# Seven products of a feed-forward pair: two PSUM regions that accumulate in turn, copied out by ScalarE in between

## The chip, the cores and the metric

The kernel runs on one core of one Trainium2 chip. The core's engines are TensorE (PE, matmuls; its weight loads are listed as PEld), VectorE (DVE), ScalarE (ACT), GpSimd (POOL) and SyncE (SP, which issues the DMAs here). The metric is the device time of one execution in microseconds (us), lower is better. Products are accumulated in PSUM, which has eight banks of 512 float32 columns per partition.

## The reference

A trunk of two layers over 512 tokens of width 1024 in float32. Each layer runs four sublayers with residuals: a feed-forward block, a mixer (gated DeltaNet in the first layer, Mamba2/SSD in the second), a cross attention to 256 memory rows, and a second feed-forward block. The change is in the feed-forward block, of which there are four:

```python
def swiglu(x, w_in, w_out):
    gate, up = jnp.split(x @ w_in, 2, axis=-1)
    return (jax.nn.silu(gate) * up) @ w_out
...
    u = swiglu(rms_norm(h, g[0, 0]), ffn_w_in[l, 0], ffn_w_out[l, 0])
    h = h + MACARON_W * rms_norm(u, g[0, 1])
```

`w_in` is 1024 x 5632 (gate and up of 2816 hidden columns each), `w_out` 2816 x 1024.

## The kernel before

Float32 operands are split into two float32r parts, `hi` and `lo`, that add up to them; ACT makes `hi` by a copy and DVE makes `lo` by a subtraction (`weights`, L129 and L130; `split`, L137 and L138). Each product is then three matmuls (`mm3`, L143 to L145: hi x hi, hi x lo, lo x hi) for each block of 128 rows.

The hidden columns of a feed-forward block come in 22 pairs of a gate and an up block of 128 columns. Pairs 0 and 1 use plain products (`plain`). The other 20 use `pair` (L473), which saves one product in eight in the manner of Strassen and Winograd: with the tokens in two halves of 256 (L, H), the 1024 rows in two halves (a, b) and gate and up as the two halves of the columns, seven products of halves give all four results. The sums of normalised rows that they need (`S1` to `S4`) are made once per block in `enter`; the sums of weights T1 to T4 are made per pair by DVE (L485, L486, L487, L489) and split (`T14`, `T23`). One product is four blocks of rows times three matmuls, twelve matmuls of 128x256 (`product`, L406).

In `pair` the products go to halves of four PSUM banks: X (tag a) takes A12 and A11, V (tag f) S2, Z (tag a) S4 and S3, Y (tag a) S1 and A22. Tag a has three banks, tag f one, s and c two each (`bank`, L113). ACT copies one result out (L502, `s5`); DVE adds the others up in SBUF:

```python
        nc.scalar.copy(self.s5, X[:, L])
        add(gt[:, L], self.s5, X[:, H])
...
        add(u2, self.s5, V[:, L])
        add(v, u2, Y[:, L])
        add(u3, u2, Z[:, H])
        sub(gt[:, H], u3, Y[:, H])
...
        add(c2(up), c2(Z), v.unsqueeze(1).broadcast_to([P, 2, 256]))
        nc.scalar.activation(gt, gt, AF.Silu)
        nc.vector.tensor_mul(gt, up, gt)
```

These are L502 to L513; then `put_hidden` splits the result (L468, L469).

Weight tiles come through three raw buffers, and five buffers each for `hi` and `lo`. `rest` (L540) walks the pairs; behind most of them it steps a generator, `slices` (L516), that multiplies two finished hidden blocks with the output weights: a chunk of 24 matmuls of 512 columns into the banks of tags s and c, for which the thresholds in `todo` decide (none behind pairs 5, 7 and 9). The order of instructions on each engine follows from dependences and from priorities that rise in the order in which the program is traced; `later` (L103) shifts the priority of a part, and `pair` has no shift.

Of the kernel before, what the change touches and what calls it, by code (L numbers as in the profile page):

```python
# [17 lines left out]
P = 128  # L18
# [43 lines left out]
class Trunk:  # L62
# [39 lines left out]
    @contextmanager  # L102
    def later(self, n):  # L103
        """what is traced here gives way to the next n instructions"""
        n = LATER.get(n, 0)
        self.tc.cur_priority += n
        yield
        self.tc.cur_priority -= n
# [4 lines left out]
    def bank(self, tag):  # L113
        """a PSUM bank: a for the long products, f, s and c for the mixers' chains"""
        return self.pm.tile([P, T], F32, name="ps_" + tag, tag=tag, bufs={"a": 3, "f": 1}.get(tag, 2))

    def weights(self, src, pool=None, nt=4):
        """a tile of weights in two float32r parts that add up to it"""
        nc = self.nc
        n = src.shape[1]  # L120
        raw = self.wp.tile([P, D], F32, name="raw", tag="raw", bufs=3)
        if pool is None:
            hi = self.wp.tile([P, D], F32R, name="whi", tag="whi", bufs=5)
            lo = self.wp.tile([P, D], F32R, name="wlo", tag="wlo", bufs=5)
        else:
            hi = pool.tile([P, D], F32R, name="thi", tag="thi", bufs=nt)
            lo = pool.tile([P, D], F32R, name="tlo", tag="tlo", bufs=nt)
        nc.sync.dma_start(out=raw[:, :n], in_=src)
        nc.scalar.copy(hi[:, :n], raw[:, :n])  # L129
        nc.vector.tensor_sub(lo[:, :n], raw[:, :n], hi[:, :n])  # L130
        return hi, lo
# [9 lines left out]
    def mm3(self, ps, lhs, rhs, first, last):  # L141
        mm = self.nc.tensor.matmul
        mm(ps, lhs[0], rhs[0], start=first, stop=False)  # L143
        mm(ps, lhs[0], rhs[1], start=False, stop=False)  # L144
        mm(ps, lhs[1], rhs[0], start=False, stop=last)  # L145
# [6 lines left out]
    def heads(self, srcs, half, st, outer=False):  # L152
        """the first products of a phase, for half of the tokens, block by block of the rows as they come"""
        if half == 0:
            st["w"] = [self.weights(x) for x in srcs]
            st["ps"] = [self.bank(x) for x in "aaaf"]
        s = slice(half * 256, half * 256 + 256)
        n = range(len(srcs))
        with self.later(0 if half else 'head'):
            for k, i in [(k, i) for i in n for k in range(KB)] if outer else [(k, i) for k in range(KB) for i in n]:  # L160
                kk = slice(k * P, k * P + P)
                w, ps = st["w"][i], st["ps"][i]
                self.mm3(ps[:, s], (w[0][:, kk], w[1][:, kk]), (self.xh[:, k, s], self.xl[:, k, s]),
                         k == 0, k == KB - 1)

    def out_weights(self, src, fh, pool=None, nt=4):
        """[[hi, lo] of each block of 128 rows] for 512 output columns"""
        res = []
        for kp in range(src.shape[1]):
            hi, lo = self.weights(src[fh, kp], pool, nt)  # L170
            for n in range(2):
                ns = slice(n * T, n * T + T)
                res.append((hi[:, ns], lo[:, ns]))
        return res

    def out(self, xs, ws, i, fh, first, last, tag):
        """u[tokens of tile i, columns of half fh] (+)= xs^T ws"""
        ps = self.bank(tag)
        ts = slice(i * P, i * P + P)
        for k, ((hi, lo), w) in enumerate(zip(xs, ws)):  # L180
            self.mm3(ps, (hi[:, ts], lo[:, ts]), w, k == 0, k == len(xs) - 1)
        nc = self.nc
        dst = self.u[:, i, fh * T:fh * T + T]
        if first:
            nc.scalar.copy(dst, ps)
        else:
            nc.vector.tensor_add(dst, ps, dst)
        if last:
            self.sumsq(dst, self.ssu[:, i, fh:fh + 1])
# [8 lines left out]
    def rcol(self, ss):  # L198
        """(mean of the squares + eps) ** -0.5, from the two sums of 512 squares"""
        nc = self.nc  # L200
        r = self.nt.tile([P, 1], F32, name="rcol", bufs=4)
        nc.vector.tensor_add(r, ss[:, 0:1], ss[:, 1:2])
        nc.scalar.activation(r, r, AF.Sqrt, bias=self.eps[:, 0:1], scale=1.0 / D)
        nc.vector.reciprocal(r, r)
        return r

    def warm(self, func, x):
        """the tables of func, loaded when x is there"""
# [10 lines left out]
    def post(self, i, square):  # L219
        """h += u * rsqrt(mean(u^2) + eps) * gain, and the sums of the squares of h"""  # L220
# [14 lines left out]
    def features(self, src, ss, g, hi, lo, ts, tag="c"):  # L235
        """the normalised rows of src [tokens, 1024], transposed, times gain g, in two parts"""
# [30 lines left out]
    def last_group(self, name, og, inner, ctx):  # L267
        """the last rows of a mixer's output projection, for the tail"""
# [12 lines left out]
    def conv(self, ps, dst, w):  # L281
        """causal taps along the tokens"""
# [6 lines left out]
    def small_proj(self, name, pool, tag, bufs):  # L289
        """the 32 columns of per-head values, [32, tokens]"""  # L290
# [10 lines left out]
    def rsqrt(self, pool, x, shape):  # L301
        """(x) ** -0.5 elementwise by Newton steps on a float32 guess; x is a small [P, n] view."""
# [12 lines left out]
    def softplus(self, pool, x, shape):  # L315
        """log1p(exp(x)) in place, as max(x, 0) + 2 atanh(e / (e + 2)) with e = exp(-|x|)."""
# [18 lines left out]
class FFN:  # L335
    """the input projection by seven products of halves (of the tokens, of the rows, gate and up) for eight"""
# [21 lines left out]
    def sums(self):  # L358
        """place for three sums of quarters of the normalised rows, in two parts"""
# [6 lines left out]
    def enter(self, i, ss, tag):  # L366
        """the normalised rows of tile i, and for the later half of the tokens the sums of quarters, in two parts"""
# [38 lines left out]
    def product(self, ps, w, x, first=True, last=True):  # L406
        """ps[feature, token] (+)= w^T x over four blocks of rows"""
        for k in range(4):
            kk = slice(k * P, k * P + P)
            self.t.mm3(ps, (w[0][:, kk], w[1][:, kk]), (x[0][:, k, :], x[1][:, k, :]), first and k == 0, last and k == 3)  # L410

    def early(self, n, ws, tags):
        """the first half of the tokens of a pair, by plain products"""
# [31 lines left out]
    def plain(self, n):  # L445
        """a pair of hidden blocks by eight products; the later half of the tokens from the sums of its quarters"""
# [26 lines left out]
    def pair(self, n):  # L473
# [5 lines left out]
        X = t.bank("a")  # L479
        for i, x in ((1, self.A12), (0, self.A11)):  # L480
            self.product(X[:, i * 256:i * 256 + 256], self.part(w, i), x)
        sub = nc.vector.tensor_sub
        T1, T4 = self.T14[:, a], self.T14[:, b]
        T2, T3 = self.T23[:, a], self.T23[:, b]
        sub(T1, u[:, a], g[:, a])  # L485
        sub(T2, u[:, b], T1)  # L486
        sub(T4, T2, g[:, b])  # L487
        w14 = t.split(self.T14)
        sub(T3, u[:, b], u[:, a])  # L489
        w23 = t.split(self.T23)  # L490
# [5 lines left out]
        up = t.nt.tile([P, T], F32, name="xs", bufs=2)  # L496
        add = nc.vector.tensor_add
        Z, Y, V = t.bank("a"), t.bank("a"), t.bank("f")
        u2, u3, v = self.s
        prods = [(V[:, L], half(w23, a), self.S2), (Z[:, L], b22, self.S4), (Y[:, L], half(w14, a), self.S1),  # L500
                 (Y[:, H], half(w14, b), self.A22), (Z[:, H], half(w23, b), self.S3)]
        nc.scalar.copy(self.s5, X[:, L])  # L502
        add(gt[:, L], self.s5, X[:, H])
        for x in prods:
            self.product(*x)
        add(u2, self.s5, V[:, L])
        add(v, u2, Y[:, L])
        add(u3, u2, Z[:, H])
        sub(gt[:, H], u3, Y[:, H])  # L509
        c2 = lambda x: x.rearrange("p (c t) -> p c t", c=2)  # L510
        add(c2(up), c2(Z), v.unsqueeze(1).broadcast_to([P, 2, 256]))
        nc.scalar.activation(gt, gt, AF.Silu)  # L512
        nc.vector.tensor_mul(gt, up, gt)  # L513
        self.put_hidden(n, gt)

    def slices(self, gi):  # L516
        """the output products of a group of hidden blocks, two blocks at a time"""
# [42 lines left out]
class DeltaNet:  # L560
# [29 lines left out]
    def rows(self, d):  # L590
        """[row][head, chunk][column] of the 8 matrices of a pair of heads in DRAM"""
        return d.rearrange("(e x) -> e x", e=8)[:, 0:P * P].rearrange("e (i j) -> i e j", j=P)

    def diag(self, d):
        """[head, chunk, block][row][column] of their diagonal blocks"""
# [19 lines left out]
    def gates(self):  # L615
        """beta, the decays' sums and what the state needs of them, per token and head."""
# [105 lines left out]
    def blocks(self, p):  # L722
        """the diagonal blocks of 16 of I + A inverted, by substitution, a block per partition"""
# [14 lines left out]
    def solve(self, p, st):  # L738
        """U = transpose of (I + A)^-1, by doubling the diagonal blocks that are inverted."""
# [425 lines left out]
class CrossAttention:  # L1165
# [21 lines left out]
    def memory(self):  # L1187
        """the normalised memory, in the place of half of the tokens"""
# [11 lines left out]
    def keys_values(self):  # L1200
        """keys [feature, slot] and values [slot, feature] of the normalised memory, to DRAM."""
# [106 lines left out]
def pack_out(w, sizes):  # L1308
    """per group of row blocks: [column half][pair of row blocks][128][2 * 512]"""
# [12 lines left out]
def pack_z(w):  # L1322
    """[1024, 2048] -> per group of 256 columns two tiles of four row blocks"""
# [114 lines left out]
```

## Time and profile before

| | us |
|---|---|
| runs, median of three | 2842.75 |
| runs, lowest and highest | 2831.45, 2849.64 |
| profiled execution, first to last instruction (span) | 2839.1 |
| PE busy in the span | 2791.8 (98%) |
| PE weight loads | 2476.0 (87%) |
| DVE busy | 2076.1 (73%) |
| ACT busy | 1520.4 (54%) |

The profile page gives the span of the profiled execution and not its device time; the runs' median is 3.65 us above it. In rows of the trace, "128x256 f32" is partitions by elements, "xN" how many instructions a row stands for, and what stands behind "|" the busy time, the mean duration in ns and the idle time of the engine just before, with the instructions that ended it. An arrow "<-" in names goes from operands to result. The ends of matmuls are modelled, and matmuls overlap.

### The profile page before, as it was taken

The page shows a single profiled execution, that of the slowest core. Times are in us where ns is not written, and L with a number is a line of the kernel's source. Part 1 is how long each engine was busy: PE and PEld are TensorE (multiplying, and loading weights), DVE is VectorE, ACT ScalarE, POOL GpSimd, SP SyncE. Part 2 cuts the span into 40 slices and gives each one's busy share as a digit, 9 for nine tenths or more (in the row PEclk, how much of TensorE's full clock was granted, in tenths as well). Part 3 has the DMA queues.
Part 4 walks back from the last instruction along what each step waited for, and adds up shares of the span by engine and source line. Part 5 has one row for each costly group of instructions (what it writes and reads, how often), then busy time and mean ns, then how long its engine had stood idle before and what let it go on. Part 6 is the DMA issues. An engine that isn't in the chain of part 4 may idle for free.

```text
span 2839.1 us, 46420 instructions
## 1 busy us (share of the span) xinstructions
PE 2791.8 (98%) x18032; PEld 2476.0 (87%) x18032; DVE 2076.1 (73%) x4057; ACT 1520.4 (54%) x2835; POOL 128.6 (5%) x141
## 2 busy tenths in 40 slices
PE   8999999999999999999999999999999999999998
PEld 7999987788878887999988999888888888799997
DVE  8887777666666565887778877777766766588776
ACT  5444486756475574544355443575554656454433
POOL 0000001000000000000000000012221200000000
PEclk9999999999999999999999999999999999999999
DMA  6333433232323532332343333433233363233233
GB/s 222 98 105 109 154 120 94 62 106 77 92 77 115 177 113 81 127 112 90 112 149 127 98 104 97 146 118 104 91 97 111 100 211 117 77 113 112 90 111 104
DMA packets 125916, 320.76 MB, mean 113 GB/s; under 512 B 27472, under 2 KB 46672, under 8 KB 125184
## 3 DMA queue, kind: packets, MB, share of 16 engines
q1 hardware_dynamic: 125696, 317.80, 34.9%
q8 instruction: 142, 2.33, 0.3%
q14 instruction: 78, 0.64, 0.1%
HBM read 293.01 MB, written 24.74 MB: 112 GB/s over the span
## 4 chain that ended last, share of the span: by engine, by line
PE 86%; DVE 8%; ACT 2%; DMA 2%; issue 1%; POOL 0%; SPq 0%; DVEq 0%; ACTq 0%
PE ps_a L143 15%; PE ps_a L144 15%; PE ps_a L145 15%; PE ps_s L144 4%; PE ps_s L145 4%; PE ps_s L143 4%; PE ps_c L145 2%; PE ps_c L143 2%; PE ps_c L144 2%; PE ps_f L145 2%; PE ps_f L144 2%; PE ps_f L143 2%; DVE h L286 1%; PE ps_s L1243 1%; PE ps_c L1068 1%
## 5 line engine op out<-in xcount | busy, mean ns | idle before, releaser
L143 PE MATMUL ps_a<-xh,whi 128*128 128x256 f32 (+1 forms) x2368 | 754.3, 321 | 2.0 <-ACT xh L381 1.7
L144 PE MATMUL ps_a<-xl,whi 128*128 128x256 f32 (+1 forms) x2368 | 754.6, 320 | 0.1
L145 PE MATMUL ps_a<-xh,wlo 128*128 128x256 f32 (+1 forms) x2368 | 752.1, 319 | 0.0
L143 PEld LDWEIGHTS ps_a<-xh,whi 128*128 128x128 f32 x2368 | 453.2, 192 | 30.4 <-ACT xh L381 2.6
L144 PEld LDWEIGHTS ps_a<-xl,whi 128*128 128x128 f32 x2368 | 454.8, 192 | 26.3 <-DVE xl L382 0.5
L145 PEld LDWEIGHTS ps_a<-xh,wlo 128*128 128x128 f32 x2368 | 454.4, 192 | 23.6
L130 DVE TENSOR_TENSOR wlo<-raw,whi 128x1024 fp32r<-128x1024 f32 x278 | 340.3, 1226 | 167.0 <-ACT whi L129 166.7
L129 ACT CAST whi<-raw 128x1024 fp32r<-128x1024 f32 x278 | 289.0, 1043 | 214.2 <-PE ps_a L144 142.0
L137 ACT CAST whi<-h 128x1024 fp32r<-128x1024 f32 x168 | 175.6, 1048 | 209.5 <-PE ps_a L144 156.5
L138 DVE TENSOR_TENSOR wlo<-h,whi 128x1024 fp32r<-128x1024 f32 x168 | 205.4, 1224 | 89.9 <-ACT whi L137 88.7
L144 PE MATMUL ps_s<-wlo,hhi 128*128 128x512 f32 x352 | 138.0, 392 | 0.0
L143 PE MATMUL ps_s<-whi,hhi 128*128 128x512 f32 x352 | 137.8, 392 | 0.0
L145 PE MATMUL ps_s<-whi,hlo 128*128 128x512 f32 x352 | 137.2, 390 | 0.0
L492 ACT CAST bh<-raw 128x512 fp32r<-128x512 f32 x80 | 49.7, 621 | 162.9 <-DMA raw<-ffn_in 135.4
L143 PE MATMUL ps_c<-whi,hhi 128*128 128x512 f32 x288 | 112.0, 389 | 0.0
L144 PE MATMUL ps_c<-wlo,hhi 128*128 128x512 f32 x288 | 112.0, 389 | 0.0
L145 PE MATMUL ps_c<-whi,hlo 128*128 128x512 f32 x288 | 112.0, 389 | 0.0
L137 ACT CAST whi<-raw 128x1024 fp32r<-128x1024 f32 x80 | 84.0, 1050 | 51.9 <-PE ps_c L145 40.8
L138 DVE TENSOR_TENSOR wlo<-raw,whi 128x1024 fp32r<-128x1024 f32 x80 | 97.6, 1220 | 9.5 <-ACT whi L137 9.4
L485 DVE TENSOR_TENSOR h<-raw 128x512 f32<-128x512 f32 x80 | 55.1, 689 | 63.9 <-DMA raw<-ffn_in 61.7
L512 ACT ACTIVATE h<-h 128x512 f32<-128x512 f32 x80 | 50.6, 633 | 81.8 <-DVE h L509 81.5
L468 ACT CAST hhi<-h 128x512 fp32r<-128x512 f32 x88 | 54.7, 622 | 70.8 <-DVE h L513 42.7
(429 smaller groups left out, 6808.2 us busy)
## 6 DMA issues: line engine op xcount, KB each, us to landing
raw<-ffn_in SPq DMA_DIRECT2D x192, 512.0 KB, 3.9
raw<-ffn_out SPq DMA_DIRECT2D x88, 512.0 KB, 3.5
raw<-dn_in SPq DMA_DIRECT2D x48, 512.0 KB, 3.6
raw<-ssd_in SPq DMA_DIRECT2D x32, 512.0 KB, 3.6
hd<-h SPq DMA_DIRECT2D x24, 512.0 KB, 3.1
h<-hd SPq DMA_DIRECT2D x24, 512.0 KB, 4.7
raw<-dn_out SPq DMA_DIRECT2D x16, 512.0 KB, 3.6
raw<-xa_k SPq DMA_DIRECT2D x16, 512.0 KB, 3.8
```

Source lines behind the costliest of these rows:

```text
L129: nc.scalar.copy(hi[:, :n], raw[:, :n])
L130: nc.vector.tensor_sub(lo[:, :n], raw[:, :n], hi[:, :n])
L137: nc.scalar.copy(hi, raw)
L138: nc.vector.tensor_sub(lo, raw, hi)
L143: mm(ps, lhs[0], rhs[0], start=first, stop=False)
L144: mm(ps, lhs[0], rhs[1], start=False, stop=False)
L145: mm(ps, lhs[1], rhs[0], start=False, stop=last)
L286: nc.vector.scalar_tensor_tensor(dst[:, j:], ps[:, 0:T - j], w[:, 3 - j:4 - j], dst[:, j:], op0=ALU.mult, op1=ALU.add)
L468: self.t.nc.scalar.copy(hi, x)
L485: sub(T1, u[:, a], g[:, a])
L492: nc.scalar.copy(b22[0], u[:, b])
L512: nc.scalar.activation(gt, gt, AF.Silu)
```

## The change

`pair` computes the same seven products in another order and with other sums. There are three regions of 256 columns, each the first half of a bank: C1 and C2 (tag a) and X (tag f). C1 takes A11 and is copied to `s5` by ACT; then S2 is added onto it and the sum is copied to `u2`; then S1, copied to `v`; then S4, after which it holds the up result of the first half of the tokens, and DVE reads it in the last product. C2 takes S3, is read for `up = v + C2`, and then A22 is added onto it for the gate of the second half. T4 has its sign turned for that. X takes A12 alone. `product` and `mm3` get an argument `again`, with which the first matmul doesn't start a new sum. `T23` is made and split ahead of `T14`. The tile `up` of the pool of tag xs goes; `up` lies where `u3` was. In the rest of the file docstrings are taken out, which moves no instruction.

```diff
-    def mm3(self, ps, lhs, rhs, first, last):
+    def mm3(self, ps, lhs, rhs, first, last, again=False):
+
         mm = self.nc.tensor.matmul
-        mm(ps, lhs[0], rhs[0], start=first, stop=False)
-        mm(ps, lhs[0], rhs[1], start=False, stop=False)
-        mm(ps, lhs[1], rhs[0], start=False, stop=last)
+        mm(ps, lhs[0], rhs[0], start=first, stop=False, skip_group_check=again)
+        mm(ps, lhs[0], rhs[1], start=False, stop=False, skip_group_check=again)
+        mm(ps, lhs[1], rhs[0], start=False, stop=last, skip_group_check=again)
...
-    def product(self, ps, w, x, first=True, last=True):
-        """ps[feature, token] (+)= w^T x over four blocks of rows"""
+    def product(self, ps, w, x, first=True, last=True, again=False):
+
+        first = first and not again
         for k in range(4):
             kk = slice(k * P, k * P + P)
-            self.t.mm3(ps, (w[0][:, kk], w[1][:, kk]), (x[0][:, k, :], x[1][:, k, :]), first and k == 0, last and k == 3)
+            self.t.mm3(ps, (w[0][:, kk], w[1][:, kk]), (x[0][:, k, :], x[1][:, k, :]), first and k == 0, last and k == 3, again)
...
         g, u = self.load(n)
         w = t.split(g)
-        X = t.bank("a")
-        for i, x in ((1, self.A12), (0, self.A11)):
-            self.product(X[:, i * 256:i * 256 + 256], self.part(w, i), x)
-        sub = nc.vector.tensor_sub
+        sub, add = nc.vector.tensor_sub, nc.vector.tensor_add
         T1, T4 = self.T14[:, a], self.T14[:, b]
         T2, T3 = self.T23[:, a], self.T23[:, b]
+        sub(T3, u[:, b], u[:, a])
         sub(T1, u[:, a], g[:, a])
         sub(T2, u[:, b], T1)
-        sub(T4, T2, g[:, b])
+        w23 = t.split(self.T23)
+        sub(T4, g[:, b], T2)
         w14 = t.split(self.T14)
-        sub(T3, u[:, b], u[:, a])
-        w23 = t.split(self.T23)
         b22 = [self.ip.tile([P, T], F32R, name="b" + x) for x in "hl"]
         nc.scalar.copy(b22[0], u[:, b])
         sub(b22[1], u[:, b], b22[0])
         half = lambda w, s: (w[0][:, s], w[1][:, s])
         gt = self.g[n % 2]
-        up = t.nt.tile([P, T], F32, name="xs", bufs=2)
-        add = nc.vector.tensor_add
-        Z, Y, V = t.bank("a"), t.bank("a"), t.bank("f")
-        u2, u3, v = self.s
-        prods = [(V[:, L], half(w23, a), self.S2), (Z[:, L], b22, self.S4), (Y[:, L], half(w14, a), self.S1),
-                 (Y[:, H], half(w14, b), self.A22), (Z[:, H], half(w23, b), self.S3)]
-        nc.scalar.copy(self.s5, X[:, L])
-        add(gt[:, L], self.s5, X[:, H])
-        for x in prods:
-            self.product(*x)
-        add(u2, self.s5, V[:, L])
-        add(v, u2, Y[:, L])
-        add(u3, u2, Z[:, H])
-        sub(gt[:, H], u3, Y[:, H])
-        c2 = lambda x: x.rearrange("p (c t) -> p c t", c=2)
-        add(c2(up), c2(Z), v.unsqueeze(1).broadcast_to([P, 2, 256]))
+        s5, u2, v = self.s5, self.s[0], self.s[2]
+        C2, C1, X = [t.bank(x) for x in "aaf"]
+        C2, C1, X = C2[:, L], C1[:, L], X[:, L]
+        self.product(C1, half(w, a), self.A11)
+        nc.scalar.copy(s5, C1)
+        self.product(C2, half(w23, b), self.S3)
+        self.product(C1, half(w23, a), self.S2, again=True)
+        nc.scalar.copy(u2, C1)
+        self.product(X, half(w, b), self.A12)
+        add(gt[:, L], s5, X)
+        self.product(C1, half(w14, a), self.S1, again=True)
+        nc.scalar.copy(v, C1)
+        up = self.s[1]
+        add(up, v, C2)
+        self.product(C1, b22, self.S4, again=True)
+        self.product(C2, half(w14, b), self.A22, again=True)
+        add(gt[:, H], u2, C2)
         nc.scalar.activation(gt, gt, AF.Silu)
-        nc.vector.tensor_mul(gt, up, gt)
+        nc.vector.tensor_mul(gt[:, L], C1, gt[:, L])
+        nc.vector.tensor_mul(gt[:, H], up, gt[:, H])
         self.put_hidden(n, gt)
```

## Rows read from the trace of the kernel before

**Rows 1.** The page's first part: busy us (share of the span) xinstructions.

```profile
span 2839.1 us, 46420 instructions
PE 2791.8 (98%) x18032; PEld 2476.0 (87%) x18032; DVE 2076.1 (73%) x4057; ACT 1520.4 (54%) x2835; POOL 128.6 (5%) x141
```

**Rows 2.** Busy by stretch: us, then PE, PEld, DVE, ACT, POOL, clock, DMA, GB/s.

```profile
46.00:341.00 295.00, 295.00 (x2094) 278.64 (x2093) 234.06 (x349) 132.78 (x172) 0.96 (x1) 1.00 0.36 114
...
1490.00:1512.00 22.00, 16.87 (x122) 15.86 (x121) 19.61 (x34) 11.02 (x20) 0.00 (x0) 0.84 0.44 144
```

**Rows 3.** Who waited for whom, 46 to 341 us: us in total, times, longest.

```profile
ACT whi L137 <- PE ps_a L144: 44.8, 30, 4.5
...
ACT whi L129 <- PE ps_c L145: 0.3, 1, 0.3
```

**Rows 4.** Timeline of PE, then ACT, about 65 us: start us, us, instruction.

```profile
64.89 0.28 PE L145 MATMUL ps_a<-xh,wlo 128*128 128x256 f32 x1
65.01 0.28 PE L143 MATMUL ps_f<-s2h,whi 128*128 128x256 f32 x1
...
65.27 0.38 ACT L502 COPY h<-ps_a 128x256 f32<-128x256 f32 x1 [0.93 <-PE ps_a L145]
```

**Rows 5.** Groups by line and form, PE, 93.25 to 103.25 us, two of thirteen.

```profile
L144 PE MATMUL ps_a<-xl,whi 128*128 128x256 f32 x16 | 4.5, 283 | 0.0
...
L143 PE MATMUL ps_f<-s2h,whi 128*128 128x256 f32 x4 | 1.1, 283 | 0.0
```

**Rows 6.** Line L502 in the first block: ns min/median/max, first and last start.

```profile
L502 ACT COPY h<-ps_a x20: 361/367/376, 50.2 to 329.7; 128x256 f32<-128x256 f32 x20
```

**Rows 7.** Groups by line and form, 46 to 341 us: DVE, then ACT.

```profile
L138 DVE TENSOR_TENSOR wlo<-h,whi 128x1024 fp32r<-128x1024 f32 x40 | 48.9, 1224 | 21.6 <-ACT whi L137 21.3
L511 DVE TENSOR_TENSOR xs<-ps_a,h 128x512 f32<-128x512 f32 x20 | 13.7, 684 | 0.0
L513 DVE TENSOR_TENSOR h<-xs,h 128x512 f32<-128x512 f32 x19 | 13.0, 685 | 0.2
L506 DVE TENSOR_TENSOR h<-h,ps_f 128x256 f32<-128x256 f32 x20 | 8.3, 415 | 0.0
...
L137 ACT CAST whi<-h 128x1024 fp32r<-128x1024 f32 x40 | 41.7, 1048 | 56.7 <-PE ps_a L144 42.3 <-DVE h L487 13.9
L502 ACT COPY h<-ps_a 128x256 f32<-128x256 f32 x20 | 7.4, 368 | 6.4 <-PE ps_a L145 6.4
```

**Rows 8.** Timeline: a chunk's weights split by DVE, and the chunk on PE.

```profile
103.02 1.23 DVE L130 TENSOR_TENSOR wlo<-raw,whi 128x1024 fp32r<-128x1024 f32 x1 [0.32 <-ACT whi L129]
...
113.37 0.40 PE L143 MATMUL ps_s<-whi,hhi 128*128 128x512 f32 x1
```

**Rows 9.** Timeline of cross attention, 1042.5 to 1044.3 us, a chain through an ACT copy.

```profile
1043.38 0.48 PE L143 MATMUL ps_a<-xh,whi 128*128 128x512 f32 x1
...
1043.67 0.37 ACT L1256 COPY pT<-ps_c 128x256 f32<-128x256 f32 x1 [0.31 <-PE ps_c L1255]
1043.70 0.40 PE L144 MATMUL ps_a<-xl,whi 128*128 128x512 f32 x1
...
1044.09 0.41 PE L1255 MATMUL ps_c<-const,p 128*128 128x128 f32 x2
```

**Rows 10.** Timeline of DeltaNet, 724 us, a chain through a DVE copy.

```profile
724.22 0.42 DVE L832 COPY w<-ps_c 128x256 f32<-128x256 f32 x1
...
724.49 0.40 PE L144 MATMUL ps_a<-xl,whi 128*128 128x512 f32 x1
...
724.72 0.69 PE L837 MATMUL ps_c<-w,gp 128*128 128x128 f32 x4
```

**Rows 11.** Busy time by stretch around a fall of the clock, columns as in rows 2.

```profile
485.00:497.00 12.00, 10.64 (x79) 8.77 (x78) 8.17 (x27) 6.67 (x20) 2.56 (x4) 1.00 0.15 45
497.00:511.00 14.00, 14.00 (x79) 9.49 (x80) 5.93 (x15) 8.00 (x29) 0.00 (x0) 0.51 0.00 0
...
700.00:800.00 100.00, 100.00 (x668) 81.01 (x667) 64.76 (x174) 54.13 (x152) 4.91 (x8) 1.00 0.31 91
```

## The prediction

> **What bounds the kernel now.** I read the engines' shares of the span first [rows 1]. PE is busy for 2791.8 of 2839.1 us; DVE for 73%, ACT for 54%. A matmul's end is modelled, so that busy share hides short gaps; the reading has to go to the stage that is changed. The table by stretch [rows 2] does that: in the first feed-forward block's stretch (46 to 341 us) PE is busy for 295.00 of 295.00 us and its weight load for 278.64, while DVE works for 234.06 and ACT for 132.78. The list of waits of that stretch [rows 3] is sorted by total, and has ACT and DVE in it, waiting for PE, for each other and for DMA, and no row of PE at all (26 rows, of which the first and the last stand there). Busy shares and waits agree: in this stage everything waits for PE, and PE for nothing.
>
> Starts are better than ends for the pace. Two matmuls of 256 columns start 0.12 us apart (64.89, 65.01), here across the change from bank ps_a to ps_f [rows 4]. A pair has seven products of twelve such matmuls; in the window of one pair without an output chunk [rows 5] every form stands with 4 or 16 of them, 84 together, and 84 x 0.12 = 10.08 us. So a product is 12 x 0.12 = 1.44 us, and the pair is nothing but its products. From the first to the last of the twenty pairs of a block 279.5 us pass (50.2 to 329.7) [rows 6].
>
> **The change part by part.** *Matmuls:* seven products before, seven after, 84 matmuls of 256 columns: 0 us. Only their order and their banks differ. The output chunks are not touched.
>
> *DVE:* removed per pair are L503, L506 to L509 (five of one form, L506's 0.415 us each: 2.075 us), L511 (0.684) and L513 (0.685): 3.44 us [rows 7]. Added are three sums of 256 columns with one operand in PSUM (3 x 0.415), a product of 256 columns with PSUM (0.415) and one from SBUF alone (between half of L513's 0.685 and 0.415; I take 0.38): 2.04 us. The difference is 1.40 us a pair, 80 pairs: 112 us of DVE. *ACT:* two more copies like L502, 0.368 us each [rows 7], 80 x 0.74 = 59 us. Neither is on the path: no PE wait stands behind DVE or ACT in these stages [rows 3], so the 112 us are worth 0, and the 59 us cost 0 as long as they delay nothing. The sums of weights (T1 to T4) and their splits stay as many; T23's comes first now. It was first needed by the third product (S2), 2.88 us into the pair, and is now needed by the second (S3), 1.44 us in. Splits run well ahead of PE (the chunk's in [rows 8] starts 10.35 us before the chunk, 103.02 against 113.37), so these 1.44 us cost 0. No DMA is added or moved; SP's queue is as it was.
>
> *New waits of PE:* C1 is written four times, and PE may not add to it until ACT has copied it. The chain is A11, copy s5, S2, copy u2, S1, copy v, S4; C2 takes A22 only after DVE has read it for `up`. From the start of a product's last matmul to the start of the copy 0.38 us pass when ACT is free (64.89 to 65.27), the copy takes 0.38 [rows 4], and a matmul follows its ACT releaser by about 0.05 (copy 1043.67 + 0.37, matmul 1044.09) [rows 9]. Together 0.80 to 0.81, of which 0.12 is the matmul's own slot: 0.68 us in which PE can't go on with C1.
> - Copy s5 has S3's product beside it, copy u2 has A12's: 1.44 us of cover against 0.68. With a whole cast of 1.05 us [rows 7] ahead of it on ACT, the copy is 1.73 us, 0.29 us too late. I take 0 (cover) and keep 0.29 for the range.
> - A22 waits for `up`: after v's copy DVE needs 0.415 us and its queue, which can hold a split of 1.22 [rows 7]. S4's product covers 1.44 us. About 0, at the worst some 0.3.
> - S4 stands right behind S1 in the program and has no cover in its own pair. This is the step that decides: 0.68 us if PE has nothing else, 80 x 0.68 = 54 us, and more where a cast is ahead.
> - The next pair starts in a third bank of tag a; its second product needs the bank that `add(gt[:, H])` frees: 0.38 + 0.415 + 0.05 against 1.44 us of A11. 0.
>
> What can PE do meanwhile? The order of instructions is made from priorities (`later` shifts them), and the trace shows that a waiting chain is filled with other matmuls. In cross attention [rows 9] PE makes a transpose, ACT copies 128x256 out of PSUM (1043.67, 0.37 us, the very form of the new copies), and PE puts two projection matmuls of 512 columns between (1043.38, 1043.70) before the next transpose (1044.09). A 512-column matmul is paced at 0.23 (724.49, 724.72 in [rows 10]). The second filler starts 0.32 after the first, whose row is longer (0.48 against 0.40) and in which I see the transposes' end, and the next transpose 0.39 after the second: the link itself lost 0.39 - 0.23 = 0.16 us, or 0.71 - 0.46 = 0.25 if both steps count. In DeltaNet [rows 10] a link through a DVE copy (L832) was filled without loss: the copy starts at 724.22 and takes 0.42, a projection matmul stands at 724.49, and the product that waited at 724.72. In the feed-forward stage the filler is the output chunk traced behind the pair, 24 matmuls of 512 columns whose weights are ready long before [rows 8]; behind a pair without a chunk (n = 5, 7 and 9 of the twenty, by the thresholds in `rest`) it is the next pair's A11 in the third bank. I take the nearest row, the ACT copy of the same shape: 0.16 us a pair.
>
> **The sum.** 80 x 0.16 = 12.8 us on the profiled execution's 2839.1: 2851.9. The runs' median, 2842.75, is 3.65 above that span, which I add as what lies around it: **2855.5 us**. A change within 1% (28 us) can hardly be told from none.
>
> **The clock.** The granted clock is full in the feed-forward stages, and falls to its 1.2 GHz level (0.51) at 497 to 511 us [rows 11]. Before that PE was busy for 10.64 of 12 us; at 700 to 800, where links are filled as above, it stayed at 1.00. So a filled link of 0.16 us in 10 us of large matmuls should not lower it. The Trainium skill (TensorE: Matmul & The Clock Gate, "A second HAM failure mode: psum-queue depth-cycling") speaks against the change here: a kernel that cycled through PSUM banks left TensorE idle for moments between groups often enough that the clock swung between its levels. By that rule the new order would bring dips; 700 to 800 us does not bear it out. As a mechanism of this kernel, one dip in each of four blocks like the one of 14 us at 497 to 511 would cost 14 / 2 = 7 us each: 4 x 7 + 12.8 = 40.8 us, 2883.5.
>
> **Rivals.**
> - *Nothing is seen* (all links filled without loss, as in [rows 10]): 2842.75.
> - *The link S1 to S4 is not filled* (slower): PE's order keeps S4 behind S1. 80 x 0.68 = 54.4 us, 2897; with ACT in a cast for 45% of the time (132.78 of 295.00 [rows 2]) and half of 1.05 us left of it, 0.68 + 0.24 = 0.92, 73.6 us, 2916. Against it: the fillers of [rows 9]. It decides over 1% when more than 28.4 / 0.68 = 42 of 80 pairs go unfilled.
> - *Copies queue behind casts*: each of s5 and u2 loses 0.29 us in 45% of the cases: 0.16 + 2 x 0.45 x 0.29 = 0.42 a pair, 33.7 us, 2876. For it: ACT is in order and its casts are 1.05 us [rows 7]. Against it: PE fills these too.
> - *Faster*: DVE's 112 us would have to show between the blocks. The stretch 1490 to 1512 [rows 2] lacks 22.00 - 16.87 = 5.1 us of PE and ran at 0.84 of the clock (22 x 0.16 = 3.5 us): at most 8.6 us, 2834, and the work there is not the pairs'.
>
> **How the numbers follow.** Forecast case 0.50 (2843 to 2870), nothing seen 0.18, unfilled 0.16, queueing 0.08, clock 0.03, faster 0.05. Slower by over 1%: unfilled 0.16, clock 0.03, over half of queueing 0.05, the tail of the forecast 0.02: 0.26. Faster by over 1%: 0.03, since no row has that much to give. Within: 0.71. The range goes from 2836 (most of the faster case and the runs' scatter, 2831.45 to 2849.64, lie out below: 0.08) to 2897 (half of the unfilled case and the worst of the others out above: 0.10).
>
> **What would show it.** Right: PE has 84 matmuls of 256 columns a pair, matmuls of an output chunk stand between S1 and S4, waits of PE on ACT in these stages are rare or under 0.2 us, DVE loses about 112 us and ACT gains 59, and a block's 279.5 us from first to last pair grow by about 19 x 0.16 = 3 us. Wrong: a row of PE waiting for ACT with 80 entries near 0.7 us (unfilled), waits at S2 and S1 (queueing), a granted clock under 1.00 inside a block, or a block of pairs that is shorter than before.

## The result: 0.56% slower, within what was forecast

The kernel after the change takes 2860.26 us (median of 6 runs, 2849.47 to 2863.22) against 2842.65 us of the kernel before, now from 6 runs: ratio 1.0056, 95% interval 1.0035 to 1.0077. That is 16 us more (10 to 22). Forecast were 2855.5 us, within 1% of before.

The page's first part after the change, the answer to [rows 1]:

```profile
span 2858.8 us, 46280 instructions
PE 2811.4 (98%) x18032; PEld 2478.2 (87%) x18032; DVE 1988.4 (70%) x3897; ACT 1574.1 (55%) x2995; POOL 126.4 (4%) x141
```

PE has the same 18032 matmuls, DVE 160 instructions fewer and ACT 160 more, two of each per pair. The table by stretch (columns as in [rows 2]) reads for the first block:

```profile
46.00:341.00 295.00, 295.00 (x2079) 275.29 (x2078) 209.31 (x306) 141.86 (x209) 0.95 (x1) 1.00 0.36 111
```

PE is still "busy" for all of 295.00 us, and yet fewer matmuls start in it (2079 for 2094), and the weight load lost 3.4 us. So this view shows that something is lost, and not where. The pairs' first and last matmul show how much. In the timeline of before the first product begins at 46.45 and the last matmul of the twentieth pair at 335.43:

```profile
46.45 0.28 PE L143 MATMUL ps_a<-xh,whi 128*128 128x256 f32 x1
...
335.43 0.28 PE L145 MATMUL ps_a<-s3h,wlo 128*128 128x256 f32 x1
```

and after it is 46.75 and 340.09:

```profile
46.75 0.28 PE L144 MATMUL ps_a<-xh,whi 128*128 128x256 f32 x1
...
340.09 0.28 PE L146 MATMUL ps_a<-xh,wlo 128*128 128x256 f32 x1
```

289.0 us have become 293.3, 4.4 us more. Of these, 0.7 us are three chunk matmuls that stood behind the last pair and now stand inside it; 3.7 us are lost, 0.18 us a pair. The row of the copy `s5` (L499 now), which answers to [rows 6], goes from 48.9 to 331.0, 282.1 us for 279.5, 2.6 us more. It is the rougher measure, since ACT does not start that copy equally late in each pair:

```profile
L499 ACT COPY h<-ps_a x20: 353/373/377, 48.9 to 331.0; 128x256 f32<-128x256 f32 x20
```

**Where in a pair.** The loss of a link is the time from one matmul's start to the next beyond the pace (0.12 us for 256 columns, 0.227 for 512); the loss of a product is the sum over its matmuls, since those behind a late start regain a few ns. Summed over the four blocks it was 0.9 us before and is 16.9 after, 15.9 us more (unrounded sums): the whole of the 16 us. The timeline of the pair at 66 us shows both places (PE and ACT rows; the ACT copy L502 is `u2`, L506 is `v`):

```profile
66.41 0.28 PE L145 MATMUL ps_a<-s2l,whi 128*128 128x256 f32 x1
66.53 0.28 PE L146 MATMUL ps_a<-s2h,wlo 128*128 128x256 f32 x1
66.65 0.28 PE L144 MATMUL ps_f<-xh,whi 128*128 128x256 f32 x1
66.73 1.05 ACT L137 CAST whi<-h 128x1024 fp32r<-128x1024 f32 x1 [2.27 <-PE ps_a L145]
...
67.68 0.37 ACT L502 COPY h<-ps_a 128x256 f32<-128x256 f32 x1
...
67.97 0.28 PE L146 MATMUL ps_f<-xh,wlo 128*128 128x256 f32 x1
68.10 0.38 PE L144 MATMUL ps_a<-xh,whi 128*128 128x256 f32 x1
...
68.32 0.28 PE L145 MATMUL ps_a<-xl,whi 128*128 128x256 f32 x1
...
69.51 0.28 PE L146 MATMUL ps_a<-xh,wlo 128*128 128x256 f32 x1
69.63 0.40 PE L144 MATMUL ps_s<-whi,hhi 128*128 128x512 f32 x1
69.83 0.37 ACT L506 COPY h<-ps_a 128x256 f32<-128x256 f32 x1 [0.61 <-PE ps_a L146]
69.86 0.40 PE L145 MATMUL ps_s<-wlo,hhi 128*128 128x512 f32 x1
...
70.10 0.39 PE L146 MATMUL ps_s<-whi,hlo 128*128 128x512 f32 x1
70.33 0.31 PE L144 MATMUL ps_a<-s4h,bh 128*128 128x256 f32 x1
...
70.47 0.28 PE L145 MATMUL ps_a<-s4l,bh 128*128 128x256 f32 x1
```

- *S4* (70.33): three chunk matmuls stand between S1 and S4, as foreseen. The second matmul of S4 follows after 0.14 us, not 0.12. Loss 0.046 us a pair, 3.1 us in the 68 pairs with a chunk behind them. In the 12 pairs without one, four matmuls of the next pair's A11 fill only 0.48 us, and the loss is 0.23 us each, 2.8 us; S4 loses 6.0 us in all. These four are then missing as cover for that pair's S3, which waits for the bank that `add(gt[:, H])` (L511) frees: 0.10 us each, 1.3 us.
- *S1* (68.10): its first row is longer (0.38) and its second matmul follows after 0.22 us: 0.10 us lost in 76 of 80 pairs, 8.0 us in all. ACT was idle for 2.27 us, then took up a cast of weights at 66.73, and `u2`'s copy stood behind it until 67.68. Both had waited for S2's product: the cast for the buffer `whi`, last read by the matmul before the last (L145 is its releaser), the copy for the sum, which the last one (L146, 66.53) completes. So the cast is ready 0.12 us earlier. In these 76 pairs the copy starts 1.15 to 1.21 us after S2's last matmul. In the other four, the first pair of each block, no cast stands ahead of it: there it starts after 0.32 us, and S1 loses nothing.
- *S2*: 0.8 us, at late starts in the first pairs of two blocks.

The rows of the next pair's S3 (behind the pair whose S4 starts at 101.61):

```profile
105.08 0.41 DVE L511 TENSOR_TENSOR h<-h,ps_a 128x256 f32<-128x256 f32 x1
...
105.55 0.38 PE L144 MATMUL ps_a<-s3h,whi 128*128 128x256 f32 x1
```

The waits of the stretch 46 to 341 us hold no row of PE after the change either, and one of the weight load, at S4:

```profile
PEld ps_a L144 <- ACT h L506: 4.1, 20, 0.3
```

S1's 0.10 us are in no list of waits: they lie within a matmul's modelled end. Only the starts show them.

### The profile page after: what moved, and what is told of

It is laid out like the page before. It is cut to its first block, busy times and chain, and to the rows that moved or that the text cites. A ratio compares the mean times of both kernels' runs of the same rounds, so it can differ in the third digit from the quotient of the medians.

```text
span 2858.8 us, 46280 instructions
## 1 busy us (share of the span) xinstructions
PE 2811.4 (98%) x18032; PEld 2478.2 (87%) x18032; DVE 1988.4 (70%) x3897; ACT 1574.1 (55%) x2995; POOL 126.4 (4%) x141
## 4 chain that ended last, share of the span: by engine, by line
PE 64%; DVE 6%; ACT 2%; DMA 1%; issue 1%; POOL 0%; DVEq 0%; ACTq 0%; SPq 0%
PE ps_a L144 12%; PE ps_a L145 11%; PE ps_a L146 11%; PE ps_s L145 4%; PE ps_s L144 3%; PE ps_s L146 3%; PE ps_c L144 2%; PE ps_c L145 2%; PE ps_c L146 2%; PE ps_f L145 1%; PE ps_f L144 1%; PE ps_f L146 1%; PE ps_s L1244 1%; PE ps_c L1069 1%; PE ps_a L1105 1%; PE ps_a L1268 1%
## 5 line engine op out<-in xcount | busy, mean ns | idle before, releaser
L144 PE MATMUL ps_a<-xh,whi 128*128 128x256 f32 (+1 forms) x2048 | 671.6, 330 | 1.2 <-ACT xh L382 1.0
L145 PE MATMUL ps_a<-xl,whi 128*128 128x256 f32 (+1 forms) x2048 | 663.6, 326 | 0.1
L146 PE MATMUL ps_a<-xh,wlo 128*128 128x256 f32 (+1 forms) x2048 | 660.9, 324 | 0.0
L144 PEld LDWEIGHTS ps_a<-xh,whi 128*128 128x128 f32 x2048 | 390.4, 191 | 34.3 <-ACT xh L382 1.9
L145 PEld LDWEIGHTS ps_a<-xl,whi 128*128 128x128 f32 x2048 | 392.6, 192 | 26.3 <-DVE xl L383 0.6
L146 PEld LDWEIGHTS ps_a<-xh,wlo 128*128 128x128 f32 x2048 | 391.9, 191 | 24.1 <-issue 0.2
L145 PE MATMUL ps_s<-wlo,hhi 128*128 128x512 f32 x352 | 138.5, 394 | 0.0
L146 PE MATMUL ps_s<-whi,hlo 128*128 128x512 f32 x352 | 137.2, 390 | 0.0
L138 DVE TENSOR_TENSOR wlo<-raw,whi 128x1024 fp32r<-128x1024 f32 x80 | 98.0, 1225 | 48.0 <-ACT whi L137 47.8
L145 PE MATMUL ps_c<-wlo,hhi 128*128 128x512 f32 x288 | 112.0, 389 | 0.0
L146 PE MATMUL ps_c<-whi,hlo 128*128 128x512 f32 x288 | 112.0, 389 | 0.0
L144 PE MATMUL ps_f<-xh,whi 128*128 128x256 f32 x384 | 109.0, 284 | 0.0
L145 PE MATMUL ps_f<-xl,whi 128*128 128x256 f32 x384 | 108.7, 283 | 0.0
```

The source lines that it names most:

```text
L138: nc.vector.tensor_sub(lo, raw, hi)
L144: mm(ps, lhs[0], rhs[0], start=first, stop=False, skip_group_check=again)
L145: mm(ps, lhs[0], rhs[1], start=False, stop=False, skip_group_check=again)
L146: mm(ps, lhs[1], rhs[0], start=False, stop=last, skip_group_check=again)
```

## The experiments

Theory: PE waits for copies of C1, at S1 since `u2`'s copy queues behind a cast, at S4 since the fillers are a little too short; DVE's relief and ACT's extra work are worth nothing. Rivals: the new load of ACT and DVE costs by itself; adding onto a sum that another engine has read costs by itself; what was lost lies outside of the pairs. "Loss" is the sum over the pace in the four blocks, in each one's profile.

**The load without the links** (`e1_loads`), from the kernel before:

```diff
...
-        add(u2, self.s5, V[:, L])
-        add(v, u2, Y[:, L])
-        add(u3, u2, Z[:, H])
-        sub(gt[:, H], u3, Y[:, H])
...
+        nc.scalar.copy(u2, V[:, L])
+        nc.scalar.copy(v, Y[:, L])
+        add(u3, v, Z[:, H])
+        add(gt[:, H], u2, Y[:, H])
...
-        nc.vector.tensor_mul(gt, up, gt)
+        nc.vector.tensor_mul(gt[:, L], Z[:, L], gt[:, L])
+        nc.vector.tensor_mul(gt[:, H], u3, gt[:, H])
```

> The products in the order and the four banks of the kernel before, none added onto another's sum; ACT and DVE do what they do after the change (three copies of 256 columns by ACT, three sums and two products of 256 columns by DVE). The sums u2, u3 and v leave out terms, so the hidden values are not the reference's. Theory (what costs is that a product of C1 waits for the copy of the one before it): no product waits, so each block's 20 pairs take 288.8 us as before and the whole about 2843 us, with DVE some 112 us less busy and ACT 59 us more. Rival (ACT's and DVE's new work, and their reads of PSUM, cost): as after the change, 292.8 us a block, 2859.

Measured: ratio 0.9997 (0.9979 to 1.0015), loss 0.9 us as before. The stretch of the first block:

```profile
46.00:341.00 295.00, 295.00 (x2097) 278.81 (x2097) 209.26 (x310) 145.64 (x213) 0.96 (x1) 1.00 0.36 113
```

DVE (209.26) and ACT (145.64) are about as busy as after the change (209.31 and 141.86) and PE starts as many matmuls as before. The load costs nothing, and DVE's relief brings nothing: what remains is the order of the sums in PSUM and the waits that it makes.

**The link not filled** (`e2_nofill`): PE's instructions of a chunk, and of the next pair, are queued behind the pair's last matmul.

```diff
-        mm(ps, lhs[1], rhs[0], start=False, stop=last, skip_group_check=again)
+        self.last = mm(ps, lhs[1], rhs[0], start=False, stop=last, skip_group_check=again)
...
-            (self.plain if n in DIRECT else self.pair)(n)
+            if n in DIRECT:
+                self.plain(n)
+                continue
+            with t.tc.issue_after(ins(t.last)) if n > 2 else ExitStack():
+                self.pair(n)
             if todo and n >= todo[0][0]:
-                next(work[todo.pop(0)[1]])
+                with t.tc.issue_after(ins(t.last)):
+                    next(work[todo.pop(0)[1]])
```

> After the change, but TensorE's order is held: matmuls of the chunk behind a pair, and of the next pair, may not go ahead of the pair's last matmul. Theory (the link S1, copy v, S4 is 0.68 to 0.73 us and is hidden by three chunk matmuls between): it shows in all 80 pairs, 80 x 0.73 = 58 us in place of the 3.7 us that the trace of after has at S4, with the 7.8 us at S1 left: 288.8 + 14.6 + 2 = 305 us a block, 2843 + 67 = 2910 us in all (2895 to 2925). Rival (the link is short and the filling doesn't matter): 2860, 293 us a block.

Measured: 2911.28 us, ratio 1.0237 (1.0206 to 1.0267), loss 67.7 us, of it 58.0 at S4 (0.72 us a pair) and 8.0 at S1. The timeline of the link and the first row of PE's list of waits for the whole run:

```profile
69.90 0.28 PE L146 MATMUL ps_a<-xh,wlo 128*128 128x256 f32 x1
70.21 0.37 ACT L510 COPY h<-ps_a 128x256 f32<-128x256 f32 x1 [0.60 <-PE ps_a L146]
...
70.64 0.39 PE L144 MATMUL ps_a<-s4h,bh 128*128 128x256 f32 x1 [0.46 <-ACT h L510]
```

```profile
PE ps_a L144 <- ACT h L510: 37.4, 80, 0.5
```

From S1's last start to the copy 0.31 us, the copy 0.37, to S4 0.06: 0.74, and 0.10 more at the matmul behind it, less the slot of 0.12. The list counts only 0.46 of the 0.72, since it begins at the modelled end. So after the change, where S4 loses 6.0 us, the fillers hide 58.0 - 6.0 = 52.0 us at S4, and the forecast's slower rival has a true price: with the links open the change costs 2.4%. The clock stayed full in the first block, as in the other three, although PE stood idle in each pair:

```profile
46.00:352.00 306.00, 296.63 (x2071) 276.08 (x2070) 206.75 (x305) 141.50 (x207) 0.95 (x1) 1.00 0.34 106
```

By the Trainium skill (TensorE: Matmul & The Clock Gate, "A second HAM failure mode: psum-queue depth-cycling") such short idle times between groups can make the clock swing; no run here shows that.

**`u2` copied by DVE** (`e3_dve`, and once more as `e3_again`):

```diff
-        nc.scalar.copy(u2, C1)
+        nc.vector.tensor_copy(u2, C1)
```

> After the change, but the copy u2 is made by DVE instead of ACT; TensorE's order stays. Theory (S1 comes 0.10 us late since copy u2 stands behind a cast of weights on ACT that becomes ready at the same moment): S1's loss of 7.8 us goes, 290.9 us a block, about 2852 us. Rival (the loss at S1 is the way from PSUM through any engine and back): as after, 292.8 us a block, 2860.

> The kernel with copy u2 by DVE once more. In its first profile the pairs took 291.0 us a block (2.0 less than after the change), yet its runs were 2859 us, and outside of the pairs it took 1698 us with 71.7 us at the lower clock. Theory (the pairs' gain is real and the rest was the clock of those executions): the median of this time is 2849 to 2856 us. Rival (the DVE copy lengthens something outside of the pairs in each execution): 2858 to 2861 again.

Measured: 2859.35 us, ratio 1.0050 (1.0030 to 1.0070), and again 2854.83 us, 1.0039 (1.0020 to 1.0058). By the time alone the first would have spoken for the rival. The loss in the pairs says otherwise: 9.9 us, 7.0 less than after the change; at S1 it fell from 8.0 to 0.5 us. The timeline:

```profile
66.99 1.05 ACT L137 CAST whi<-h 128x1024 fp32r<-128x1024 f32 x1 [2.16 <-PE ps_a L145]
...
67.11 0.42 DVE L502 COPY h<-ps_a 128x256 f32<-128x256 f32 x1 [0.78 <-PE ps_a L146]
...
68.35 0.28 PE L144 MATMUL ps_a<-xh,whi 128*128 128x256 f32 x1
...
68.47 0.28 PE L145 MATMUL ps_a<-xl,whi 128*128 128x256 f32 x1
```

The cast still starts first, the copy 0.12 us later on another engine, and S1's matmuls are back at 0.12 us. The cause of S1's loss is thereby shown: the queue on ACT. Outside of the pairs (the span less the pair matmuls and chunks of the four blocks at the pace, 4 x 288.65 us, and less their loss) the first profile was 1698 us, the second 1688, with 10.7 us of loss in the pairs. The 2852 us expected of the first run were missed for what lies outside; the last section sets its runs beside the others at the same clock.

**A22 between S1 and S4** (`e5_covered`), in the third bank of tag a:

```diff
-        C2, C1, X = [t.bank(x) for x in "aaf"]
-        C2, C1, X = C2[:, L], C1[:, L], X[:, L]
+        C2, C1, X, Y = [t.bank(x) for x in "aafa"]
+        C2, C1, X, Y = C2[:, L], C1[:, L], X[:, L], Y[:, L]
...
-        self.product(C1, b22, self.S4, again=True)
-        self.product(C2, half(w14, b), self.A22, again=True)
-        add(gt[:, H], u2, C2)
+        self.product(Y, half(w14, b), self.A22)
+        self.product(C1, b22, self.S4, again=True)
+        add(gt[:, H], u2, C2)
+        add(gt[:, H], gt[:, H], Y)
```

> After the change, but A22's product has a bank of its own (the third of tag a) and stands between S1 and S4; DVE adds it to u2 + C2 afterwards. So each product of C1 has another product's 1.44 us between it and the one before. Theory (loss at S4 is the part of its link that three chunk matmuls, 0.68 us, don't cover, and at pairs without a chunk more): the losses at S4 (3.7 us) and of the pairs without a chunk (3.0 us) go, S1's 7.8 stay: 291.0 us a block, 2852 us. Rival (adding onto a sum that another engine has read costs by itself): as after, 292.8 us a block, 2860.

Measured: 2853.27 us, ratio 1.0037 (1.0021 to 1.0054), loss 9.7 us: nothing at S4 nor at pairs without a chunk, and 8.0 us at S1 as it was. A sum added onto a copied one costs nothing once another product stands between.

**Both covers** (`e7_both`): the edits of the last two together.

> After the change with both covers: copy u2 made by DVE, and A22 in a bank of its own between S1 and S4. Theory (the loss is the sum of the two late links and nothing else): both losses go, the pairs of a block take 288.9 to 289.3 us, as before (288.8), and the whole is 2840 to 2847 us. Rival (adding onto a copied sum, or ScalarE's reads of C1, cost something that covering doesn't hide): 291 us a block or more, 2852 and above.

Measured: 2847.71 us, ratio 1.0016 (1.0002 to 1.0030), loss 2.3 us. The pairs are back at the pace of before: from the first product to the last matmul of the twentieth pair 288.8 us pass (289.0 before):

```profile
46.90 0.28 PE L144 MATMUL ps_a<-xh,whi 128*128 128x256 f32 x1
...
335.74 0.28 PE L146 MATMUL ps_a<-s4h,bl 128*128 128x256 f32 x1
```

The median is 0.7 us above what was expected, with 1.4 us more of loss in the pairs than before; the interval begins at 0.6 us. A gain over the kernel before is not in it: PE had no gap to give in this stage.

**The copy of S1's sum made twice** (`e6_twice`):

```diff
+        junk = t.nt.tile([P, T], F32, name="xs", bufs=2)
+        nc.scalar.copy(junk[:, L], C1)
         nc.scalar.copy(v, C1)
```

> After the change with the copy of S1's sum made twice by ACT (once to a place that nobody reads), so the link S1 to S4 is about 0.27 to 0.37 us longer. Theory (the order of instructions is made so that other matmuls fill the link): four chunk matmuls stand between in place of three (0.91 us for about 1.0 to 1.1 us), the loss at S4 grows to 0.1 to 0.2 us a pair, 2864 to 2872 us. Rival (the filling is fixed and TensorE pays for the second copy): 80 x 0.27 to 0.37 = 22 to 30 us more, 2882 to 2890.

Measured: 2862.14 us, ratio 1.0070 (1.0048 to 1.0091), just under what was expected. The loss is 20.0 us; at S4 it grew from 6.0 to 8.0 us, not by 22 to 30, and in the pairs without a chunk from 0.10 to 0.17 us at the next pair's S3, which lacks seven matmuls of A11 as cover instead of four. The second copy starts 0.27 us after the first, and four chunk matmuls stand in the link instead of three:

```profile
69.44 0.40 PE L144 MATMUL ps_s<-whi,hhi 128*128 128x512 f32 x1
69.64 0.37 ACT L507 COPY xs<-ps_a 128x256 f32<-128x256 f32 x1 [0.61 <-PE ps_a L146]
...
69.91 0.38 ACT L508 COPY h<-ps_a 128x256 f32<-128x256 f32 x1
...
70.14 0.40 PE L144 MATMUL ps_s<-whi,hhi 128*128 128x512 f32 x1
...
70.38 0.35 PE L144 MATMUL ps_a<-s4h,bh 128*128 128x256 f32 x1
```

In all 68 pairs with a chunk the number of fillers is the same (three after the change, four here): the order follows the length of the link, in steps of 0.23 us.

**The kernel before, profiled again** (`before_again`):

> The kernel before, profiled a second time. Theory (outside of the pairs the profiles differ by where the granted clock falls in an execution, not by the change): pairs 288.8 us a block again, while the time outside of them differs from the first profile's 1684 us by several us, along with the time at the lower clock (37.6 us there). Rival (what lies outside is the same in each execution): 1684 us within 1 us.

Measured: 2843.16 us in the one run, span 2841.4; loss in the pairs 0.9 us again, and 1685.9 us outside of the pairs for 1683.6, with 47.8 us at the lower clock for 37.6. The two differ by 2.3 us, more than the rival's 1 and less than the "several" of the theory; the last section puts it beside the other profiles.

## Why the prediction was right, and where it was not

- *What bounds the stage* held: e1_loads has the lighter DVE and the busier ACT and takes the time of before. The work taken from DVE was overestimated: 112 us forecast, 2076.1 - 1988.4 = 88 us measured, because the rows of short DVE instructions overlap (70.42 and 70.75 are the starts of two neighbours after the change, 0.33 us apart with 0.41 us in the row). The durations of all DVE rows, added up, fell by 109 us, from 2294.6 to 2185.6, close to the forecast. ACT's 59 us are 1574.1 - 1520.4 = 54.
- *The link S1 to S4* was named as the step that decides, at 0.68 us if open and 0.16 if filled. Open it is 0.72 us (e2_nofill). Filled it is 0.05 us, and 0.23 at pairs without a chunk: 6.0 us for the forecast 12.8. The mechanism was right and the term too large by more than twice: the row of cross attention that it was taken from had two fillers for a link of the same length, and here are three.
- *Copies s5 and u2 under another product's cover* were put at 0, with 0.29 us kept for a cast ahead. This is the term that failed: at S1 it is 0.10 us a pair, 8.0 us, the largest part of the loss. The prediction counted a cast ahead as chance, by ACT's busy share (45%; the casts of 1.05 us alone are 86 of the 295 us, 29%). It is no chance: S2's last two matmuls set free first the buffer that a cast waits for and then, 0.12 us later, the sum that the copy waits for, and so the cast goes first in nearly every pair. e3_dve shows it: there the cast starts at 66.99 and DVE's copy at 67.11. It costs 0.10 us and not 0.29, because a cast that became ready 0.12 us before the copy delays it by less than its whole length: from S2's last matmul to the copy 1.15 us pass and not 0.32, so it is 0.83 us late.
- *The next pair's bank* was put at 0; it costs 0.10 us at the 12 pairs without a chunk, 1.3 us: four of A11's twelve matmuls had been used up at S4, and DVE's add came 0.62 us after A22's last matmul (104.46), not 0.38.
- The sum, 12.8 forecast and 15.9 measured in the pairs, was near by luck: one term was too large and another too small.
- *The clock* stayed at 1.00 in the blocks, as expected. DVE's relief showed nowhere outside of the pairs, so the faster rival fell. The reading of 700 to 800 us was weak: in four later profiles a fall of 17.1 us begins between 725 and 798 us (in e2_nofill the clock is 0.51 from 725 to 742), so one profile's full clock there says little.
- "Waits of PE on ACT are rare or under 0.2 us" was right, but a poor test: the larger loss is in no list of waits.

## What to carry to other kernels

When an engine has no gap in a stage, lighter work on the others buys nothing there, and a new wait behind it costs what the order of instructions can't fill. A region that is read out between two additions to it needs another product between them, longer than matmul to copy, copy, and back (0.74 us here for 256 columns), and the copy needs an engine on which nothing longer becomes ready by the same product. Look for such losses in the starts of matmuls, since busy shares and waits hide up to a matmul's modelled end.

## What the runs showed of the hardware

The order of PE's, DVE's and ACT's instructions between the blocks is the same in all these kernels, yet the time outside of the pairs went from 1676.8 us (e6_twice) to 1697.9 us (e3_dve). It goes with the time for which the granted clock was at 1.2 GHz between start and end: 23.9 us in the one and 71.7 us in the other, 0.44 us for each; a line through all ten profiles has 0.41 us for each and misses none by more than 1.2 us. In the first profile of before it was 37.6 us, and the two longest falls lay at 497 to 511 and 921 to 934 us ([rows 11] has the first); in the second one, of the same program, one came at 463 us:

```profile
451.00:463.00 12.00, 11.94 (x124) 9.12 (x123) 9.37 (x20) 5.35 (x13) 2.00 (x2) 1.00 0.53 149
463.00:477.00 14.00, 14.00 (x60) 10.29 (x61) 7.25 (x26) 5.81 (x12) 0.00 (x0) 0.51 0.19 70
```

So a pair of profiles compares well inside the feed-forward blocks and only to some 10 us as a whole. The medians of e2_nofill, e3_dve, e5_covered and e7_both lie 3 to 10 us above what their loss in the pairs adds to before. The clock that is on record for each run explains most of it. Within the runs of one kernel, 0.001 of mean clock goes with 2.3 us (118 runs). Set to a clock of 0.991 by that slope, the kernels' mean times lie above that of before as far as their loss in the pairs does, to within 1.5 us:

| kernel | us above before at equal clock | loss in the pairs above before |
|---|---|---|
| after | 16.1 | 15.9 |
| e1_loads | -0.3 | 0.0 |
| e2_nofill | 68.0 | 66.8 |
| e3_dve, e3_again | 10.0, 9.2 | 9.0, 9.8 |
| e5_covered | 10.2 | 8.8 |
| e6_twice | 19.4 | 19.1 |
| e7_both | 2.9 | 1.4 |

The 2859 us of e3_dve were thus mostly its runs' lower clock (0.9896 on the mean, before 0.9923). Whether the last 1 to 1.5 us of e2_nofill, e3_dve, e5_covered and e7_both are more than scatter stays open.
